# An FFN up projection by seven half products instead of eight, with the norm ahead of the products

## The chip, the cores and the metric

The kernel runs on one core of a Trainium2 chip. The metric is the device time of one execution in microseconds (us). The engines are TensorE (PE, with its weight loads PEld), VectorE (DVE), ScalarE (ACT), GpSimd (POOL) and SyncE (SP), whose queue issues nearly all DMAs.

## What is computed

Two layers of an encoder over 768 tokens, 512 of one sequence and 256 of another. A layer adds a merge of four gated branches to x, and then a feed-forward network (FFN) with a depthwise convolution of width 3 along the tokens:

```python
def rms_norm(x, g):
    xf = x.astype(jnp.float32)
    y = xf * lax.rsqrt(jnp.mean(xf * xf, axis=-1, keepdims=True) + EPS)
    return (y * g.astype(jnp.float32)).astype(x.dtype)

def conv_ffn(h, w_up, w_dw, b_dw, w_down):
    u = depthwise_conv(h @ w_up, w_dw, b_dw)
    a, b = jnp.split(u, 2, axis=-1)
    return (jax.nn.silu(a) * b) @ w_down
...
        x = x + merged @ w_out[l]
        x = x + conv_ffn(rms_norm(x, ffn_norm[l]), ffn_w_up[l], ffn_conv_w[l], ffn_conv_b[l], ffn_w_down[l])
```

The model has 1024 features, and the FFN 2816 for each of a and b. All is float32.

## The kernel before

**Layout.** Features lie on the 128 partitions and tokens along the free dimension; x, h and the products are 8 blocks of 128 features by 768 tokens. Sequence one has columns 0 to 511, sequence two 512 to 767. A float32 product is three products of parts: an operand is split into `hi` and `lo`, and `fm` issues for each block k of 128 features `wh` x `xh`, `wh` x `xl` and `wl` x `xh` (L377), each on 512 columns and then on 256 (`full`). So one output block of 128 features takes 8 x 3 x 2 = 48 matmuls, into a PSUM tile `mm` of two banks.

**Weights** are streamed in units of 512 columns (four blocks): SP loads `raw`, ScalarE casts it to `whi` (`put_hi`, L332), VectorE makes `wlo` (`put_lo`, L338). `pump` emits these when the main stream, whose advance in microseconds is estimated as products are emitted, says that they are due. Ten pairs and five raw tiles are held. Small work (side streams) is written as generators, whose steps are emitted in between products in the same way; an engine's queue then runs in the order of emission.

**Norm.** h is x times the gains, not normalised; `x_in` makes its parts and the sums of squares as x becomes final. The factor 1/rms of each token (`rbc`, in the rows as `ssq`) multiplies what the products give.

**FFN.** There are 22 pairs j: column block j gives a, column block 22 + j gives b. `ffn_half` makes one block: 48 matmuls, VectorE multiplies PSUM by `rbc` (L1208), ScalarE writes the middle tap and bias (L1201) into `u`, and VectorE adds the side taps (L1195, L1197) from PSUM, for each sequence in its turn. `ffn_glu` then makes silu(a) b: tanh on ScalarE, a VectorE step (L1235), GpSimd's product (L1236), and a split (L1238, L1240). The order of up groups and down products is `FF_ORDER`; a down product is done two up groups later than its up group where there are such (d0 after u1). `FF_GROUPS` are (0, 2), (2, 4), (6, 4), (10, 4), (14, 4), (18, 4). A down adds into x, which stays in SBUF (L1267); the last of a layer gives the next layer's h, or the output. `lagged` makes the last blocks of a product sequence one first, so that the next stage can start on it, and `ffn_first` starts on sequence one in the same way.

**Around it.** `proj_out` is the output projection ahead of the FFN. Its last five blocks go through `lagged`, each product in a small PSUM tile of its own.

Of the kernel before, what the change touches and what calls it, by code (L numbers as in the profile page):

```python
# [23 lines left out]
NFF = 22  # L24
FF_GROUPS = ((0, 2), (2, 4), (6, 4), (10, 4), (14, 4), (18, 4))
FF_ORDER = ("u0", "u1", "d0", "u2", "d1", "u3", "d2", "u4", "d3", "u5", "d4", "d5")
# [27 lines left out]
def layer_units(i, l):  # L54
# [34 lines left out]
    for step in FF_ORDER:  # L89
        j0, n = FF_GROUPS[int(step[1])]  # L90
        if step[0] == "u":
            for j in range(j0, j0 + n):
                out.extend(fu[j])
                out.extend(fu[NFF + j])
        else:
            w = wd[128 * j0:128 * (j0 + n)]
# [79 lines left out]

class Units:
    """The operands in the next n units of the weights, each w columns wide, taken from the stream when first asked
    for."""
# [16 lines left out]
class Net:  # L196
    """One pass through the layers. The large products (the main stream) are emitted in order; the rest of a
    branch (side streams) is written as generators whose steps are emitted between them, and a step's yield says
    how much of the main stream (in microseconds of the tensor engine) comes before its next one."""

    WB = 10
    RB = 5
    T_HI = 3.0
    T_LO = 0.7
    NB = 24

    def __init__(self, ctx, tc, depth, widths, xin, wu, mcd, fcd, mud, hcd, out):
# [15 lines left out]
        self.raws, self.his, self.ready = [], [], []  # L223
        self.nrm = {}

# [14 lines left out]
    def phase(self, name, ns, nmm):  # L240
        """The pools of a phase: ns small tiles, nmm of the wide PSUM tiles."""
# [56 lines left out]
    def drain(self, e=None):  # L298
        """Emit side steps until e is done (all of them without e)."""
# [6 lines left out]
    def pump(self):  # L306
        """Emit what is due: a unit's load, its hi part once the load should have come, then its lo part."""
        more = True
        while more:
            more = False  # L310
            if self.his and self.his[0][0] + self.T_LO <= self.now:
                self.put_lo()
                more = True
            if self.raws and self.live < self.WB and self.raws[0][0] + self.T_HI <= self.now:
                self.put_hi()
                more = True
            self.load_raw()

    def load_raw(self, most=RB):
        while self.di < self.depth * len(self.widths) and len(self.raws) + len(self.his) < most:  # L320
# [4 lines left out]
            self.raws.append((self.now, n, raw))  # L325
            self.di += 1

    def put_hi(self):
        _, n, raw = self.raws.pop(0)
        self.live += 1  # L330
        hi = self.pw.tile([128, n], F32R, tag="whi", name=self.nm("whi"), bufs=self.WB)
        self.nc.scalar.copy(hi, raw)  # L332
        self.his.append((self.now, n, raw, hi))

    def put_lo(self):
        _, n, raw, hi = self.his.pop(0)
        lo = self.pw.tile([128, n], F32R, tag="wlo", name=self.nm("wlo"), bufs=self.WB)
        self.nc.vector.tensor_sub(lo, raw, hi.bitcast(F32))  # L338
        self.ready.append((hi, lo))

    def unit(self):
        while not self.ready:
            if self.his:
                self.put_lo()
            else:
                self.load_raw()
                self.put_hi()
# [1067 lines left out]
```

## Time and profile before

| | |
|---|---|
| runs | 2823.68, 2825.2, 2837.93 us; median 2825.2 |
| span of the profiled execution, which is the time of that execution too | 2825.7 us |
| TensorE busy | 2788.8 us, 99% |
| VectorE busy | 1624.0 us, 57% |
| ScalarE busy | 949.5 us, 34% |
| GpSimd busy | 482.8 us, 17% |
| DMA, share of 16 engines | 20% |
| matmuls | 15676 with the transposes |

The page cuts the span in 40 slices and prints for each engine the busy share in tenths. The chain that ended last is followed back from the last instruction, at each step to what released it. Windows give busy times in stretches of the span with the granted clock of TensorE; the groups by form give count, busy time and mean duration of one kind of instruction; the timeline gives instructions in order of time.

### The profile page before, as it was taken

What the parts mean: (1) busy time and instruction counts of PE and PEld (TensorE: products, weight loads), DVE (VectorE), ACT (ScalarE), POOL (GpSimd) and SP (SyncE); (2) the same over time, 40 slices, a digit from 0 to 9 for tenths busy, and PEclk for the clock granted to TensorE, in tenths of its full rate; (3) what the DMA queues carried; (4) which work ended last, traced back from release to release, by engine and by line L of the source; (5) the groups of instructions that cost most, each with busy time, mean ns of one, the idle gap of its engine ahead of it and who ended that gap; (6) DMA issues with size and microseconds to landing.
All of it is one profiled execution on the core that took longest, in us unless ns stands there. A gap on an engine that the chain in (4) does not pass through costs nothing.

```text
span 2825.7 us, 39870 instructions
## 1 busy us (share of the span) xinstructions
PE 2788.8 (99%) x15676; PEld 2428.6 (86%) x15676; DVE 1624.0 (57%) x2804; ACT 949.5 (34%) x1929; POOL 482.8 (17%) x408
## 2 busy tenths in 40 slices
PE   9999999999999999999999999999999999999999
PEld 8778988888888888888787789888888888888888
DVE  6644438886445665555446443387874466655653
ACT  6443333223233332223344433342232333322330
POOL 3402113121121010000114021231121210100000
PEclk9999999999999999999999999999999999999999
DMA  5101113221132211221221011132212221212211
GB/s 166 42 27 38 41 47 114 61 67 60 60 105 62 67 64 60 64 64 56 81 91 42 27 38 31 57 110 64 62 62 64 90 75 61 68 60 68 64 59 58
DMA packets 110204, 183.35 MB, mean 65 GB/s; under 512 B 16321, under 2 KB 32065, under 8 KB 110017
## 3 DMA queue, kind: packets, MB, share of 16 engines
q1 hardware_dynamic: 110016, 180.81, 20.2%
q8 instruction: 123, 2.02, 0.3%
q14 instruction: 65, 0.52, 0.1%
HBM read 168.03 MB, written 11.16 MB: 63 GB/s over the span
## 4 chain that ended last, share of the span: by engine, by line
PE 94%; DVE 3%; POOL 1%; ACT 1%; issue 1%; DMA 0%; SPq 0%; ACTq 0%; DVEq 0%; POOLq 0%
PE mm L377 61%; PE mm L397 16%; PE ps L377 8%; PE ps L386 3%; PE ps L856 2%; PE ps L673 1%; PE ps L904 1%; PE ps L706 1%; PE ps L907 1%; POOL st L404 0%; DVE wlo L338 0%; PE ps L620 0%; PE ps L463 0%; PE ps L397 0%; PE ps L622 0%
## 5 line engine op out<-in xcount | busy, mean ns | idle before, releaser
L377 PE MATMUL mm<-hh,whi 128*128 128x256 f32 (+1 forms) x2560 | 668.0, 340 | 1.2 <-ACT whi L332 1.2
L332 ACT CAST whi<-raw 128x512 fp32r<-128x512 f32 (+1 forms) x576 | 354.3, 616 | 924.7 <-PE mm L377 779.2
L377 PE MATMUL mm<-hh,wlo 128*128 128x256 f32 (+1 forms) x2560 | 664.0, 338 | 0.0
L377 PE MATMUL mm<-hl,whi 128*128 128x256 f32 (+1 forms) x2560 | 661.7, 337 | 0.0
L338 DVE TENSOR_TENSOR wlo<-raw,whi 128x512 fp32r<-128x512 f32 (+1 forms) x576 | 419.7, 737 | 97.4 <-ACT whi L332 95.6
L377 PEld LDWEIGHTS mm<-hh,whi 128*128 128x128 f32 x2560 | 394.5, 188 | 60.8 <-issue 3.5
L377 PEld LDWEIGHTS mm<-hh,wlo 128*128 128x128 f32 x2560 | 393.8, 188 | 55.9
L377 PEld LDWEIGHTS mm<-hl,whi 128*128 128x128 f32 x2560 | 392.1, 188 | 55.9
L377 PE MATMUL mm<-b,whi 128*128 128x512 f32 (+1 forms) x1600 | 351.4, 339 | 7.0 <-DVE b L1151 6.2
L397 PE MATMUL mm<-whi,hh 128*128 128x512 f32 (+2 forms) x752 | 311.6, 414 | 7.3 <-ACT hh L422 6.1
L377 PEld LDWEIGHTS mm<-b,whi 128*128 128x128 f32 x1600 | 248.0, 190 | 46.4 <-DVE b L1151 4.9
L397 PE MATMUL mm<-whi,hl 128*128 128x512 f32 (+2 forms) x752 | 278.2, 370 | 0.0
L397 PE MATMUL mm<-wlo,hh 128*128 128x512 f32 (+2 forms) x752 | 277.7, 369 | 0.0
L1236 POOL TENSOR_TENSOR s<-s,s 128x768 f32<-128x768 f32 x44 | 91.3, 2076 | 890.6 <-DVE s L1235 890.6
L377 PE MATMUL mm<-b,wlo 128*128 128x512 f32 (+1 forms) x800 | 212.6, 340 | 0.0
L397 PEld LDWEIGHTS mm<-whi,hh 128*128 128x128 f32 x752 | 177.1, 235 | 29.2 <-issue 11.2
L404 POOL TENSOR_TENSOR st<-st,mhalf 128x16 f32<-128x16 f32 (+4 forms) x46 | 90.7, 1971 | 590.9 <-DVE st L781 372.3
L377 PE MATMUL ps<-b,whi 128*128 128x512 f32 (+1 forms) x832 | 189.7, 338 | 0.0
L397 PEld LDWEIGHTS mm<-wlo,hh 128*128 128x128 f32 x752 | 179.1, 238 | 11.8 <-issue 4.6
L397 PEld LDWEIGHTS mm<-whi,hl 128*128 128x128 f32 x752 | 177.4, 236 | 11.5 <-DVE hl L429 0.5
L1135 POOL TENSOR_TENSOR b<-b,b 128x768 f32<-128x768 f32 x48 | 99.8, 2078 | 462.3 <-DVE b L1130 437.4
L1008 DVE SCALAR_TENSOR_TENSOR b<-b,mc,b 128x497 f32<-128x497 f32 (+14 forms) x240 | 170.7, 760 | 0.1
(183 smaller groups left out, 3129.6 us busy)
## 6 DMA issues: line engine op xcount, KB each, us to landing
raw<-wu SPq DMA_DIRECT2D x560, 256.0 KB, 2.6
do<-ot SPq DMA_DIRECT2D x36, 132.0 KB, 2.4
b<-do SPq DMA_DIRECT2D x12, 384.0 KB, 3.5
raw<-wu SPq DMA_DIRECT2D x16, 208.0 KB, 2.8
b<-xin SPq DMA_DIRECT2D x8, 384.0 KB, 6.5
b<-xsp SPq DMA_DIRECT2D x8, 384.0 KB, 6.3
out<-b SPq DMA_DIRECT2D x8, 384.0 KB, 2.3
b<-xin SPq DMA_DIRECT2D x8, 256.0 KB, 5.0
```

Source lines behind the costliest of these rows:

```text
L332: self.nc.scalar.copy(hi, raw)
L338: self.nc.vector.tensor_sub(lo, raw, hi.bitcast(F32))
L377: nc.tensor.matmul(ap, w, x[:, c0:c1], start=(k == 0 and i == 0), stop=(k == K - 1 and i == 2))
L386: self.nc.tensor.transpose(out, x, self.ident)
L397: nc.tensor.matmul(ap, x[:, cols], w, start=(k == 0 and i == 0), stop=(k == 7 and i == 2))
L404: self.nc.gpsimd.tensor_tensor(r, ms, self.mhalf[:, 0:n], op=ALU.pow)
L673: nc.tensor.matmul(sc[:, 0:S], qkT[hh][:, 128 * t:128 * t + 128], qkT[4 + hh][:, 128 * t0:128 * t0 + S], start=True, stop=True)
L706: nc.tensor.matmul(sh["po"][:, hh, :], PT[:, 128 * kb:128 * kb + 128], v[(t0 + kb) // 3][:, (t0 + kb) % 3, 64 * hh:64 * hh + 64], start=(k ...
L856: nc.tensor.matmul(sc[:, x, y, 0:W], qT[y][rr, 128 * t:128 * t + 128], kT[y][rr, k0:k0 + W], start=True, stop=True)
L1008: nc.vector.scalar_tensor_tensor(acc[f][:, o0:o1], hc[f][:, o0 + d:o1 + d], w[:, 31 * f + k:31 * f + k + 1], acc[f][:, o0:o1], op0=ALU.mul ...
L1135: nc.gpsimd.tensor_add(a, a, t)
L1236: nc.gpsimd.tensor_mul(t, t, b)
```

## The change

**Seven products for eight.** Write the weights of a pair as blocks a11, a12 (column block j, features 0 to 511 and 512 to 1023) and a21, a22 (column block 22 + j), and h as b11, b21 (its two feature halves for columns 0 to 383) and b12, b22 (columns 384 to 767). A half product takes 4 blocks k of features on 384 columns: 12 matmuls. A pair takes eight of them in the usual way. `ffn_seven` takes seven, by Strassen's scheme in Winograd's form, on sums of weight blocks (s1 = a21 + a22, s2 = s1 + a11, s4 = s2 + a12, a21 + a11; the signs lie in the operands and in the last additions) and on operands T1 to T4 that are made once per layer from h:

```diff
+    def ffn_seven(self, j):
...
+        p = self.mm_ps()
...
+        X, Y = p[:, 0:HALF], p[:, 512:512 + HALF]
+        z1, z2 = self.s(NT), self.s(NT)
...
+        prod(X, b11)
+        nc.scalar.copy(z1[:, a], X)
+        prod(Y, b21)
+        nc.vector.tensor_add(z1[:, a], z1[:, a], Y)
+        self.ffn_rest()
+        Z = self.mm_ps()[:, 0:HALF]
+        prod(Z, self.tx["T1"])
+        nc.scalar.activation(z2[:, b], Z, AF.Identity, scale=-1.0)
+        prod(X, self.tx["T2"], True)
+        nc.scalar.copy(z1[:, b], X)
+        prod(Z, b22, True)
+        nc.vector.tensor_add(z1[:, b], z1[:, b], Z)
+        del Z
+        u1 = self.ffn_u(z1, j)
+        del z1
+        prod(X, self.tx["T3"], True)
+        nc.vector.tensor_sub(z2[:, b], z2[:, b], X)
+        self.rest = (j, X, z2, u1)
+
+    def ffn_rest(self):
...
+        self.fm(((X, 0, HALF),), self.units(1, 128), self.tx["T4"], 4, more=True)
+        self.nc.scalar.activation(z2[:, 0:HALF], X, AF.Identity, scale=-1.0)
+        del X
+        u2 = self.ffn_u(z2, NFF + j)
+        del z2
+        self.ffn_gate(j, u1, u2)
```

`more=True` goes on adding to what the PSUM tile holds. The last product of a pair, T4, is `ffn_rest`: it is issued in the next pair behind Y, or directly where a down product comes next. The results are put together in SBUF (`z1`, `z2`), and `ffn_u` makes the taps from there: `ffn_mid` (L1419 now) and `ffn_conv` (L1413, L1415 now) read SBUF. The lines of the PSUM steps are L1485 to L1509; the gate's VectorE steps are L1520 and L1525, GpSimd's product L1521.

**The order** is now a list; pairs 0 and 1 (`FF_PLAIN`) keep eight half products, 20 pairs per layer take seven:

```diff
-FF_ORDER = ("u0", "u1", "d0", "u2", "d1", "u3", "d2", "u4", "d3", "u5", "d4", "d5")
+FF_PLAIN = 2
+HALF = NT // 2
+
+FF_SEQ = (("u", 0), ("u", 1), ("u", 2), ("u", 3), ("d", 0, 2), ("u", 4), ("u", 5), ("u", 6), ("d", 2, 4), ("u", 7),
+          ("u", 8), ("u", 9), ("u", 10), ("d", 6, 4), ("u", 11), ("u", 12), ("u", 13), ("u", 14), ("d", 10, 4),
+          ("u", 15), ("u", 16), ("u", 17), ("u", 18), ("u", 19), ("d", 14, 4), ("u", 20), ("u", 21), ("d", 18, 4))
```

**Weights.** The stream gets a step between load and cast, a list of feeds; `L409` is the line of the sums, of which s1 and s4 are GpSimd's and the other two VectorE's. A pair that had four units of `hi` and `lo` has seven. The line of `put_hi` is L418 and that of `put_lo` L427. Eight pairs and six raw tiles are held, and three sums.

```diff
+        out += [
+            Feed("sum", a21, a22, s1, pool, last=a22),
+            Feed("sum", s1, a11, s2, dve, done=(s1,), last=a22),
+            Feed("sum", s2, a12, s4, pool, done=(s2, s4, a12), last=a22),
+            Feed("in", a21, a11, None, dve, done=(a21, a11), last=a22),
+        ]
```

**Norm ahead.** `hnorm_gen` waits for the sums of squares of 384 columns, makes `rbc`, and then for each k one VectorE product (L585), ScalarE's cast (L455) and VectorE's `lo` (L456). `t_gen` makes T1 to T4 in the same way, 16 operands, all emitted before pair 2; T2's difference is in part GpSimd's. `proj_out` works on halves of 384 columns, its last four blocks two to a PSUM tile, and calls `hnorm` after each half.

```diff
+        for k in range(8):
+            h = self.xs[k][:, cols]
+            nc.vector.scalar_tensor_tensor(h, h, g[:, k:k + 1], self.rbc[:, cols], op0=ALU.mult, op1=ALU.mult)
+            self.split(self.hs[k][0][:, cols], self.hs[k][1][:, cols], h)
+            yield 1.1
...
+        for k in range(4):
+            nc.vector.tensor_sub(x1[k][:, a], x1[k][:, a], x1[k][:, b])
+            t12[k] = self.b(dt=F32R), self.b(dt=F32R)
+            self.split(t12[k][0][:, a], t12[k][1][:, a], x1[k][:, a])
+            self.tx["T1"].append(tuple(t[:, a] for t in t12[k]))
+            yield 1.0
```

`ffn_plain` makes the first three column blocks half by half, with the results copied to SBUF (`flat`, L1433), and ends with `run_out`, which emits what is left of `t_gen`.

**x in DRAM.** The tiles of x hold h and its combinations during the FFN, so x goes to DRAM (`save_x`) after the projection and after each down, and a down loads it block by block into three buffers:

```diff
+                for m in range(8):
+                    if m < 7:
+                        load(m + 1)
...
+                    x = xr.pop(m)
+                    nc.vector.tensor_add(x, x, p[:, 0:NT])
+                    if last:
+                        nc.sync.dma_start(out=self.out[m], in_=x)
+                    else:
+                        self.go_fast(self.save_x(m, x, 0, NT), 1.5)
```

The last down of a layer issues the products of all but its last operand for some blocks first (`early`), and then waits for the side streams.

**Where instructions stand now.** VectorE in the middle of the first FFN, one column block of before: `mm` is the product in PSUM, `s` the small tiles with u, `b` x.

```order
L1208 TENSOR_TENSOR mm_8705<-mm_8705,ssq_7259 128x768
L1195 SCALAR_TENSOR_TENSOR s_8704<-mm_8705,fc_80,s_8704 128x511
L1197 SCALAR_TENSOR_TENSOR s_8704<-mm_8705,fc_80,s_8704 128x511
L1195 SCALAR_TENSOR_TENSOR s_8704<-mm_8705,fc_80,s_8704 128x255
L1197 SCALAR_TENSOR_TENSOR s_8704<-mm_8705,fc_80,s_8704 128x255
L338 TENSOR_TENSOR wlo_8781<-raw_8600,whi_8764 128x512
L1235 SCALAR_TENSOR_TENSOR s_8785<-s_8785,s_8630 128x768
L1267 TENSOR_TENSOR b_7278<-b_7278,mm_8774 128x768
```

No product of TensorE waits for one of these but through a free PSUM tile. VectorE after the change, at the end of a group, ahead of a down: s_9039 is `z1`, s_9040 `z2`, mm_9038 the tile of X, mm_9106 that of Z.

```order
L1495 TENSOR_TENSOR s_9039<-s_9039,mm_9106 128x384
L1413 SCALAR_TENSOR_TENSOR s_9169<-s_9039,fc_80,s_9169 128x511
L1415 SCALAR_TENSOR_TENSOR s_9169<-s_9039,fc_80,s_9169 128x511
L1413 SCALAR_TENSOR_TENSOR s_9169<-s_9039,fc_80,s_9169 128x255
L1415 SCALAR_TENSOR_TENSOR s_9169<-s_9039,fc_80,s_9169 128x255
L1525 SCALAR_TENSOR_TENSOR b_9105<-s_9117,b_9104 128x768
L427 TENSOR_TENSOR wlo_9182<-raw_9049,whi_9166 128x512
L1500 TENSOR_TENSOR s_9040<-s_9040,mm_9038 128x384
```

L1500, which reads T3's result out of X's tile, stands behind the taps of z1 and the gate's `lo` of the pair before. TensorE of before, where the up columns end and a down begins:

```order
L377 MATMUL mm_8705<-hl_7277,whi_8408 128x512
L377 MATMUL mm_8705<-hl_7277,whi_8408 128x256
L377 MATMUL mm_8705<-hh_7276,wlo_8424 128x512
L377 MATMUL mm_8705<-hh_7276,wlo_8424 128x256
L377 MATMUL mm_8774<-b_8052,whi_8446 128x512
L377 MATMUL mm_8774<-b_8052,whi_8446 128x256
```

The down goes into another PSUM tile. The same place after the change: `hh`, `hl` are T3's operands (they have taken the place of h's), `b_8263`, `b_8264` T4's.

```order
L472 MATMUL mm_9038<-hh_7258,whi_9007 128x384
L472 MATMUL mm_9038<-hl_7259,whi_9007 128x384
L472 MATMUL mm_9038<-hh_7258,wlo_9023 128x384
L472 MATMUL mm_9038<-b_8263,whi_9035 128x384
L472 MATMUL mm_9038<-b_8264,whi_9035 128x384
L472 MATMUL mm_9038<-b_8263,wlo_9047 128x384
```

T4's matmuls follow T3's, in the same PSUM tile, which L1500 reads in between. VectorE of before at the FFN's start, between the first two column blocks' second sequences and the next block (ssq is `rbc`):

```order
L1225 TENSOR_TENSOR mm_7901<-mm_7901,ssq_7259 128x256
L1195 SCALAR_TENSOR_TENSOR s_7899<-mm_7901,fc_80,s_7899 128x255
L1197 SCALAR_TENSOR_TENSOR s_7899<-mm_7901,fc_80,s_7899 128x255
L338 TENSOR_TENSOR wlo_8062<-raw_7879,whi_8046 128x512
L1235 SCALAR_TENSOR_TENSOR s_8066<-s_8066,s_7898 128x768
```

Only taps, gates and weights stand there. After the change, at the first pair with seven products, s_8279 is its `z1`, and L619 and L456 make T4's operands, the last of sixteen:

```order
L619 SCALAR_TENSOR_TENSOR b_7282<-b_7282 128x384
L456 TENSOR_TENSOR b_8272<-b_7282,b_8271 128x384
L427 TENSOR_TENSOR wlo_8287<-raw_7903,whi_8234 128x512
L1520 SCALAR_TENSOR_TENSOR s_8289<-s_8289,s_8128 128x768
L427 TENSOR_TENSOR wlo_8308<-raw_7832,whi_8297 128x512
L1487 TENSOR_TENSOR s_8279<-s_8279,mm_8278 128x384
```

L1487, the add of Y, stands behind all operands.

## Rows read from the trace of the kernel before

**Rows 1.** The page: span, shares and 40 slices of TensorE and its clock.

```profile
span 2825.7 us, 39870 instructions
PE 2788.8 (99%) x15676; PEld 2428.6 (86%) x15676; DVE 1624.0 (57%) x2804; ACT 949.5 (34%) x1929; POOL 482.8 (17%) x408
...
PE   9999999999999999999999999999999999999999
...
PEclk9999999999999999999999999999999999999999
```

**Rows 2.** The page: the chain that ended last, by engine and line.

```profile
PE 94%; DVE 3%; POOL 1%; ACT 1%; issue 1%; DMA 0%; SPq 0%; ACTq 0%; DVEq 0%; POOLq 0%
PE mm L377 61%; PE mm L397 16%; PE ps L377 8%; PE ps L386 3%; PE ps L856 2%; PE ps L673 1%; PE ps L904 1%; PE ps L706 1%; PE ps L907 1%; POOL st L404 0%; DVE wlo L338 0%; PE ps L620 0%; PE ps L463 0%; PE ps L397 0%; PE ps L622 0%
```

**Rows 3.** Windows in layer 1's FFN: length, busy (instructions) per engine, clock, DMA.

```profile
2280.00:2820.00 540.00, 539.58 (x3115) 471.37 (x3115) 306.82 (x432) 152.13 (x212) 45.64 (x22) 1.00 0.19 63
2640.00:2700.00 60.00, 60.00 (x348) 52.46 (x347) 32.06 (x44) 14.85 (x22) 4.00 (x2) 1.00 0.20 62
```

**Rows 4.** Timeline, `lagged` of layer 0's end: start, duration, engine, line, tiles.

```profile
1379.85 0.39 PE L377 MATMUL mm<-b,wlo 128*128 128x512 f32 x1
1380.27 0.69 DVE L1151 TENSOR_TENSOR b<-b,mm 128x512 f32<-128x512 f32 x1 [1.27 <-PE mm L377]
...
1381.02 0.50 PE L377 MATMUL mm<-b,whi 128*128 128x512 f32 x1 [0.78 <-DVE b L1151]
```

**Rows 5.** Groups by form, ScalarE: count, busy us, mean ns, idle before.

```profile
L332 ACT CAST whi<-raw 128x512 fp32r<-128x512 f32 x560 | 345.7, 618 | 905.8 <-PE mm L377 764.6 <-issue 63.3 <-PE mm L397 62.2
L1238 ACT ACTIVATE b<-s 128x768 fp32r<-128x768 f32 x44 | 37.2, 846 | 159.4 <-POOL s L1236 159.4
L629 ACT COPY b<-ps 128x384 f32<-128x384 f32 x12 | 5.7, 478 | 30.4 <-PE ps L620 30.4
```

**Rows 6.** Timeline of VectorE in layer 1's FFN, from a block's first side tap.

```profile
2598.68 0.75 DVE L1195 SCALAR_TENSOR_TENSOR s<-mm,fc,s 128x511 f32<-128x511 f32 x1 [1.06 <-ACT s L1201]
...
2601.04 1.28 DVE L338 TENSOR_TENSOR wlo<-raw,whi 128x512 fp32r<-128x512 f32 x2
```

**Rows 7.** Groups by form, VectorE.

```profile
L1235 DVE SCALAR_TENSOR_TENSOR s<-s,s 128x768 f32<-128x768 f32 x44 | 41.8, 951 | 0.0
L612 DVE TENSOR_TENSOR b<-b,st 128x384 f32<-128x384 f32 x24 | 16.2, 714 | 0.4 <-POOL st L404 0.4
L861 DVE TENSOR_TENSOR s<-ps,hc 128x384 f32<-128x384 f32 x16 | 8.9, 555 | 44.9 <-PE ps L856 44.9
```

**Rows 8.** Groups by form, GpSimd: the gate product, and a sum of 512 columns.

```profile
L1236 POOL TENSOR_TENSOR s<-s,s 128x768 f32<-128x768 f32 x44 | 91.3, 2076 | 890.6 <-DVE s L1235 890.6
L432 POOL TENSOR_TENSOR ssq<-ssq,s 128x512 f32<-128x512 f32 x28 | 37.5, 1339 | 141.0 <-ACT s L427 140.8
```

**Rows 9.** GpSimd beside L1008: timeline, the line's minimum/median/maximum there, and undisturbed form.

```profile
549.72 2.17 POOL L1135 TENSOR_TENSOR b<-b,b 128x768 f32<-128x768 f32 x1 [8.10 <-DVE b L1130]
...
L1008 DVE SCALAR_TENSOR_TENSOR b<-b,mc,b x3: 469/733/2331, 550.1 to 553.3; 128x508 f32<-128x508 f32 x1, 128x252 f32<-128x252 f32 x1, 128x507 f32<-128x507 f32 x1
...
L1008 DVE SCALAR_TENSOR_TENSOR b<-b,mc,b 128x505 f32<-128x505 f32 x8 | 5.9, 737 | 0.0
```

**Rows 10.** The page: DMA issues, KB each, median us to landing.

```profile
b<-do SPq DMA_DIRECT2D x12, 384.0 KB, 3.5
...
out<-b SPq DMA_DIRECT2D x8, 384.0 KB, 2.3
```

**Rows 11.** Window behind 1414 us, after gaps in `lagged`; the clock is third from the end.

```profile
1416.00:1421.00 5.00, 4.49 (x21) 4.19 (x21) 2.04 (x6) 1.93 (x5) 2.33 (x4) 0.50 0.51 150
```

More of the change, by code (lines that the diff above doesn't have):

```diff
@@ L174, in layer_consts, with __init__, layer_feeds, plain @@
     return c, f, np.concatenate([uq, ukv, sln, ws], axis=1)
+class Feed:
+    def __init__(self, out, a, b=None, name=None, eng=None, done=(), last=0):
+        self.out, self.a, self.b, self.name, self.eng = out, a, b, name, eng
+        self.done, self.last = done, last
+def layer_feeds(l, widths):
+    n = len(widths)
+    n_ff = sum(4 if x[0] == "u" else 2 * x[2] for x in FF_SEQ)
+    out, late = [], []
+    pool, dve = (lambda nc: nc.gpsimd), (lambda nc: nc.vector)
+    def plain(u):
+        return Feed("raw", u, done=(u,), last=u)
+    u = l * n
+    out += [plain(u + i) for i in range(n - n_ff)]
+    u += n - n_ff
+    for step in FF_SEQ:
+        if step[0] == "d" or step[1] < FF_PLAIN:
+            c = 2 * step[2] if step[0] == "d" else 4
+            out += late
+            late = []
+            out += [plain(u + i) for i in range(c)]
+            u += c
+            continue
+        a11, a12, a21, a22 = range(u, u + 4)
+        s1, s2, s4 = (f"s{x}_{u}" for x in (1, 2, 4))
+        out += [Feed("raw", a11, last=a11), Feed("raw", a12, last=a12)] + late
+        out += [
[4 more added lines that the diff above has]
+        ]
+        late = [plain(a22)]
+        u += 4
+    assert u == l * n + n and not late
+    return out
 class Units:
@@ L324, in load_raw, with can_sum, t_due @@
             self.nc.sync.dma_start(out=raw, in_=self.wu[l, i, :, 0:n])
-            self.raws.append((self.now, n, raw))
+            self.raws[self.di] = raw
+            self.t_raw[self.di] = self.now
             self.di += 1
+    def can_sum(self):
+        if self.fs >= len(self.feeds):
+            return False
+        f = self.feeds[self.fs]
+        return f.last < self.di and not (f.out == "sum" and len(self.sums) >= self.SB)
+    def t_due(self):
+        return self.t_raw[self.feeds[self.fs].last] + self.T_HI
@@ new lines, in put_src @@
+    def put_src(self):
+        f = self.feeds[self.fs]
+        if f.out == "raw":
+            self.src[self.fs] = self.raws[f.a]
+            self.t_src[self.fs] = self.now
+        else:
+            a = self.sums[f.a] if isinstance(f.a, str) else self.raws[f.a]
+            b = self.raws[f.b]
+            if f.out == "sum":
+                o = self.pw.tile([128, 512], F32, tag="sum", name=self.nm("sum"), bufs=self.SB)
+                self.sums[f.name] = o
+            else:
+                o = a
+            f.eng(self.nc).tensor_add(o, a, b)
+            self.src[self.fs] = o
+            self.t_src[self.fs] = self.now + self.T_SUM
+        self.fs += 1
@@ L376, in fm @@
                 for ap, c0, c1 in segs:
[L377 removed]
+                    nc.tensor.matmul(ap, w, x[:, c0:c1], start=(k == 0 and i == 0 and not more),
+                                     stop=(k == K - 1 and i == 2), skip_group_check=more)
             if rel and k % rel == rel - 1:
```

328 lines of the change are left out of this document (240 added, 88 removed).

## The prediction

> **What bounds the kernel now.** I read the page's shares and slices first: TensorE is busy 99% of the span, in every slice, at the full granted clock (2.4 GHz) [rows 1]. The chain that ended last says the same: 94% of it is matmuls, and the product helper's line L377 leads [rows 2]. Then the windows of the FFN: in 540 us TensorE idles 0.42 us, and Vector works 307 of them [rows 3]. So the FFN is bound by TensorE, and each matmul that is taken out is worth its time so long as TensorE stays fed. 60.00 us hold 348 matmuls, half of 512 columns and half of 256, so 172.4 ns for a mean of 384 columns [rows 3].
>
> Span and page are 2825.7, 0.5 above the median of 2825.2; the sum is made against 2825.7 and 0.5 comes off.
>
> **The saving.** A pair of up columns takes 4 x 4 x 3 x 2 = 96 matmuls of mean 384 columns, 16.55 us. Seven half products take 7 x 12 = 84 of 384 columns, 14.48 us (2.07 each). 40 pairs change, so TensorE's own work falls by 40 x 2.07 = **82.8 us**. What follows is what it waits for instead.
>
> **Y waits for the copy of X.** X and Y lie in one PSUM tile, and Y's first matmul waits for ScalarE's copy out of X's half. The nearest row is a product that waited for Vector to read its tile's other half: the matmul after it started 1.17 us later instead of 0.23, 0.94 lost [rows 4]. Scalar's copy of 384 columns is 478 ns against that add's 687 [rows 4, 5], so I take 0.72; between 0 (not waited for) and 0.94. Seven plus this wait: 15.20 us.
>
> **Vector's queue in one pair.** Per seven it runs 7 weight `lo` parts (two in 1.28 us [rows 6], so 4.48), two weight sums (1.28), three adds out of PSUM (0.555 each [rows 7], 1.67), eight side taps (four in 2.36, from 2598.68 to 2601.04 [rows 6]; 4.72) and two gate operations (0.951 [rows 7]; 1.90): **14.05 us**. So far it fits under 15.20. Two things come on top. The side taps now read both inputs from SBUF while GpSimd runs: s1 and s4 (about 1.34 each) and the gate product of 2.08 [rows 8]. The trace has that meeting: a 508-wide operation of two SBUF inputs, started at 550.10 while a GpSimd product of 2.17 ran from 549.72, took 2331 ns where 505 columns take 737 undisturbed [rows 9], so 1.59 is lost. I charge one such loss for the gate product and 0.9 for s4. And the taps of z1 wait until Scalar has made the middle tap, which stands behind a `hi` cast of 0.85 and a weight cast of 0.62 [rows 5]: 1.2. The period is then 14.05 + 1.59 + 0.9 + 1.2 = **17.75 us**; it replaces 15.20, since T2 waits for Vector's add of Y and T4 for its subtraction L1500 (the order of Vector's queue above). From below 15.6 (14.05 with one loss), from above 19.3 (both sums lose 1.59 and the middle tap 0.4 more).
>
> By the Trainium skill ("SBUF — State Buffer", Who interferes with whom), a Vector instruction with two SBUF inputs contends with a GpSimd instruction that reads SBUF and the later comer waits for all of it; one with at most one SBUF input does not. It speaks against this change, which moves the taps' input from PSUM to SBUF; by it all 4.76 us of GpSimd could stand in Vector's way instead of my 2.49, which is the third rival below. The 1.59 lost of 2.17 [rows 9] agrees with it.
>
> **The end of a group.** Before each down product T4 follows T3 directly. T4 needs L1500, and in Vector's queue that stands behind the add of Z, four taps, the gate's `lo` and a weight's `lo`. From the end of b22: add 0.555, middle tap 0.85, taps 2.36, 0.95, 0.64, L1500 0.555, with hand-overs of 0.2 at four places 6.7; T3 covers 2.07 of it. So TensorE stands still **at least 4.6 us**, 12 times (55 us), and longer when Vector comes late: with a last period of 17.2 it is 6.9.
>
> **The groups.** After a down the first seven takes 13.2; X, the wait and Y of the next, 4.86; T4 2.07: T4 of the first ends at 20.1. A group of n ends at 20.1 + 17.75 (n - 2) + 17.2, against 16.55 n before: +4.2 for n = 2, +5.4 for 3, +6.6 for 4, +7.8 for 5. A layer has 2, 3, 4, 4 and 5 behind its first down: **+30.6**. These numbers hold the saving already.
>
> **From the output projection to the first down.** Here h is normalised before any product can start. One k is a Vector product (0.714, the row of two SBUF inputs), Scalar's cast (0.478) and Vector's `lo` (0.555) in a row: 1.75 [rows 5, 7]. Count from the end of the projection's first half. The first half's chain (add, square, GpSimd's sum, small matmuls, power, broadcast, copy) takes about 6.2, an estimate from rows of 0.5 to 1.7 each; eight k's with four `lo` parts and two adds between them end at 24.0, and the last add of the second half stands in Vector's queue behind seven of them, at 22.2. The second chain then ends at 22.2 + 6.2 + 14.0 = 42.4, and the third plain column at 42.4 + 0.5 + 8.3 = 51.2; TensorE's work till there is 41.3. Next come the operands T1 to T4, all emitted ahead of j = 2, and T2 of j = 2 waits for the add of Y behind all of them: copies and taps 5.0, T1 7.0, T2 7.0, T3 2.2, T4 7.0, with taps, gate, sums and `lo` parts between 8.5, so **36.7 us**, of which 14.4 lie beside TensorE's fourth column, X and Y. Then 28.1 remain to the down. 51.2 + 36.7 + 28.1 = 116.0 against 16.55 x 5 = 82.8: **+33.2 per layer**. Between +20 (k's at 0.555 for the product, and operands that overlap) and +42 (GpSimd's losses in each k).
>
> **x in DRAM.** Per down eight loads and eight saves of 384 KB join SP's queue, with 3.5 and 2.3 us [rows 10] against 4.1 us of TensorE per block where n = 4: nothing, hidden by the block before. In d(0,2) a block has 2.07 and three buffers turn in about 6.8: I charge 1.5 per layer (0 to 5). Layer 0's and 1's ends, with operands needed at once: 1.5 each.
>
> **The clock.** After TensorE idled and waited around 1414 us, the granted clock was 0.50 (1.2 GHz) there, and 21 matmuls of 256 columns took 4.49 us where they take 2.5 [rows 11]. The stalls of 5 to 22 us above are longer than the gaps there. 12 times 1.7, so **20 us**; 0 to 40.
>
> **Sum.** 2 x (30.6 + 33.2) + 2 x 3 + 20 = 154 on 2825.7: 2979, less 0.5. **2979 us.**
>
> **The rivals.**
> (a) TensorE stays the bound: **faster**. Place: the add of Y, the copy of X and L1500 come through Vector's queue without a wait. For it: Vector's 14.05 lies under 15.20 and it has 43% of the span free today. Against it: the chain of 6.7 at a group's end. The price: 40 x 0.2 for Y, 12 x 2 for T4, 10 per layer for the start: 8 + 24 + 20 - 82.8 = -31, so 2794. It decides from the point where all added waits lie under 2.07 per pair.
> (b) Vector's queue holds only its own sum: the period is 15.6 and the last one 14.95 (stall 4.6), the start +20, no clock loss. Groups come to +2.4 per layer: 2 x (2.4 + 20 + 1.5) + 2825 = 2873; with half of the clock loss and +28 at the start, 2900.
> (c) GpSimd's ports and the long start weigh more: period 19.3, last 18.7, start +42, clock 40: 2 x (50.7 + 42 + 1.5) + 40 + 2825 = 3053.
> (d) It does not do what it says: products are fewer but as slow as before, with the waits hidden: near 2825.
>
> **How the numbers follow.** My forecast (2930 to 3015) 0.53; (b), 2860 to 2930, 0.21; (c), 3015 to 3090, 0.15; (a) 0.07; (d) 0.04. The range takes in the bounds 2873 and 3053: 2872 to 3055. Faster by over 0.5% (14 us, about what a measurement of this kernel can tell from none) 0.07, within it 0.04, slower 0.89.
>
> **What would show it.** In the changed profile TensorE's share falls to about 90% and its idle time names Vector: L1487, L1500, L585/L456 and the copy L1485. The matmul of Y after X starts 0.5 to 0.9 late, 40 times; before each down there is a gap of 5 to 7 us; T2 of j = 2 has a gap of some 22 us; T4 to T4 within a group takes 17 to 18 us. If Vector idles between its rows while TensorE works, (a) or (b) is right; if the taps of 511 take 2 us where GpSimd runs, (c). Wrong would be the forecast if the chain at a group's end is under 4 us, or if the operands T1 to T4 are made at under 1.2 us per k.

## The result

The changed kernel takes **3071.7 us** (3068.4 to 3073.4) against 2824.4: 1.086 of the time before (95% interval 1.083 to 1.089). The forecast was 2979, with a range of 2872 to 3055. The sign was right, and the time lies 17 us above the range.

The page of the changed kernel, in the form of [rows 1]: span, shares, and the slices of TensorE and of its clock.

```profile
span 3068.7 us, 40394 instructions
PE 2775.4 (90%) x15196; PEld 2487.2 (81%) x15196; DVE 1837.2 (60%) x3118; ACT 1097.9 (36%) x2245; POOL 622.3 (20%) x496
...
PE   9999999999974798898899999999999757988988
...
PEclk9999999999997999999999999999999979999999
```

TensorE's share has fallen from 99 to 90%, as forecast. The hole does not lie evenly in the FFN: in each layer there is one slice with 7, one with 4 or 5 and another with 7, at the FFN's start, and from there on 8 and 9.

TensorE's waits by releaser (us in total, times, longest us):

```profile
PE mm L472 <- ACT s L1485: 113.1, 40, 33.5
PE mm L472 <- DVE s L1500: 98.0, 28, 10.4
PE mm L472 <- DVE b L1379: 20.5, 10, 5.8
PE mm L472 <- DVE xr L1571: 9.4, 6, 3.5
```

L1485 is the copy of X, for which Y waits (40 times, as forecast), L1500 the subtraction for which T4 waits, L1379 the adds in the output projection's halves, L1571 the add of a down. Windows in both FFNs, in the form of [rows 3] (540 us, busy us per engine, clock, DMA):

```profile
900.00:1440.00 540.00, 433.58 (x2355) 404.36 (x2354) 365.14 (x516) 204.24 (x334) 103.93 (x60) 0.93 0.32 104
2430.00:2970.00 540.00, 434.17 (x2351) 404.73 (x2350) 363.67 (x516) 204.67 (x335) 104.52 (x60) 0.93 0.31 103
```

TensorE idles 106 us of 540, where it idled 0.4 before [rows 3].

**Where the 243 us are** that lie between the two profiled executions (3068.7 and 2825.7). The stretch ahead of the first FFN runs the same work in all kernels, but its end (the last cast ahead of the projection) lies between 784.0 and 790.6 us in 13 profiles. To be free of that, I count from there: before 2041.6 us to the end, the changed kernel 2278.9, so **+237**. Within that, by the starts of a down's last add in layer 1 (2557.74, 2865.09 and others in the timeline) against before's pace of 99.8 us for four pairs and a down:

| layer 1 | before, same work | after | difference | forecast |
|---|---|---|---|---|
| projection to the first down's end (4 pairs) | 153.5 | 235.4 | **+81.9** | +36.4 |
| 3 pairs and down | 83.2 | 89.9 | +6.7 | +7.1 |
| 4 pairs and down | 99.8 | 109.2 | +9.4 | +8.3 |
| 4 pairs and down | 99.8 | 108.3 | +8.5 | +8.3 |
| 5 pairs and down | 116.4 | 127.7 | +11.3 | +9.5 |
| 2 pairs and the layer's end | 66.5 | 71.2 | +4.7 | +7.4 |

(The forecast's column takes its clock term, 1.7 per stall, and its 1.5 for the ends into the rows.) The five groups come to +40.6 where +40.6 was forecast; to the tenth that is luck, since the rows miss by up to 2.7 either way. In layer 0 the start costs +83 and the groups about +31: before takes 101.8 us there for four pairs and a down (why is open), the changed kernel 107.6 and 108.2, no more than in layer 1. So it is the FFN's start that was missed, by 45 us or a little more in each layer.

**A pair inside a group.** Each takes 17.4 us:

```profile
1382.60:1400.00 17.40, 15.12 (x84) 14.48 (x84) 15.60 (x23) 8.96 (x16) 4.45 (x2) 1.00 0.19 62
```

VectorE is busy 15.6 of the 17.4. From the timeline of the second half of this pair, by engine:

```profile
1391.45 2.94 DVE L427 TENSOR_TENSOR wlo<-sum,whi 128x512 fp32r<-128x512 f32 x2
1394.31 0.54 DVE L1495 TENSOR_TENSOR s<-s,mm 128x384 f32<-128x384 f32 x1
1396.19 0.75 DVE L1413 SCALAR_TENSOR_TENSOR s<-s,fc,s 128x511 f32<-128x511 f32 x1 [1.34 <-ACT s L1419]
...
1393.87 0.85 ACT L1523 ACTIVATE b<-s 128x768 fp32r<-128x768 f32 x1 [3.22 <-POOL s L1521]
...
1391.61 2.23 POOL L1521 TENSOR_TENSOR s<-s,s 128x768 f32<-128x768 f32 x1 [4.88 <-DVE s L1520]
```

GpSimd's gate product starts at 1391.61. The two weight parts on VectorE beside it take 2.94 where two take 1.28 undisturbed [rows 6]: 1.66 lost, where I had charged 1.59 (on the taps, which come later). The Trainium skill ("SBUF — State Buffer", Who interferes with whom) names VectorE's second SBUF input as what meets GpSimd's reads; the 1.66 agree.

VectorE then waits 1.34 for the middle tap of z1 (L1419). Scalar's cast L1523, which waits for GpSimd, stands ahead of that tap, but it is not what makes the wait: the tap needs the add of Z, and with the cast behind the tap (x8) VectorE still waits 1.10, as it does without GpSimd's product (x7, x11). The cast has 0.24 of it.

**Ahead of a down**, T3's last matmul and T4's first:

```profile
1410.99 0.34 PE L472 MATMUL mm<-hh,wlo 128*128 128x384 f32 x1
1418.00 1.01 PE L472 MATMUL mm<-b,whi 128*128 128x384 f32 x2 [6.67 <-DVE s L1500]
```

7.01 us from start to start, so 6.8 lost; 6.9 were forecast.

**The FFN's start** in layer 0. First the chain from the last add of the projection's first half (838.80) to the first normalised block:

```profile
838.80 0.55 DVE L1379 TENSOR_TENSOR b<-b,mm 128x384 f32<-128x384 f32 x1 [4.61 <-PE mm L472]
...
840.10 1.03 POOL L550 TENSOR_TENSOR ssq<-ssq,s 128x384 f32<-128x384 f32 x1 [4.16 <-ACT s L548]
842.24 0.72 PE L564 MATMUL ps<-ones,ssq 128*128 128x1 f32 x6
843.00 0.16 DVE L567 TENSOR_SCALAR st<-ps 128x3 f32<-128x3 f32 x1 [0.95 <-PE ps L564]
843.24 0.87 POOL L503 TENSOR_TENSOR st<-st,mhalf 128x3 f32<-128x3 f32 x1 [2.11 <-DVE st L567]
844.72 1.46 DVE L573 TENSOR_SCALAR s<-hc,st 128x128 f32<-128x128 f32 x3
848.01 0.81 PE L576 MATMUL ps<-s,ones 128*128 128x384 f32 x2
850.45 0.46 ACT L580 COPY ssq<-ps 128x384 f32<-128x384 f32 x1
850.95 1.17 DVE L585 SCALAR_TENSOR_TENSOR b<-b,fc,ssq 128x384 f32<-128x384 f32 x1 [0.40 <-ACT ssq L580]
```

12.1 us, and the second half's chain (866.97 to 879.34) 12.4, where 6.2 were forecast. The steps take 6.6 us; between them stand gaps of up to 1.8 us, above all around the small matmuls, which take their turn among TensorE's products: GpSimd's sum ends at 841.1 and L564 starts at 842.24, the diagonal is done at 846.2 and L576 starts at 848.01. The product of the projection's second half halts meanwhile, since the add for which it waits stands in VectorE's queue behind the blocks:

```profile
853.19 0.34 PE L472 MATMUL mm<-b,wlo 128*128 128x384 f32 x1
859.37 1.01 PE L472 MATMUL mm<-b,whi 128*128 128x384 f32 x2 [5.85 <-DVE b L1379]
```

Then the operands. Y of the first pair waits for the copy of X:

```profile
946.89 0.51 ACT L455 CAST b<-b 128x384 fp32r<-128x384 f32 x1 [1.09 <-DVE b L619]
...
948.57 0.47 ACT L1485 COPY s<-mm 128x384 f32<-128x384 f32 x1
...
949.09 0.69 PE L472 MATMUL mm<-hh,whi 128*128 128x384 f32 x1 [33.47 <-ACT s L1485]
```

X was done at 915. Its copy stands in Scalar's queue behind the sixteenth operand's cast (946.89), so TensorE stands still for 33.5 us.

### The profile page after: what moved, and what is told of

Its sections match the earlier page's. It is cut to its first block, busy times and chain, and to the rows that moved or that the text cites. A ratio compares the mean times of both kernels' runs of the same rounds, so it can differ in the third digit from the quotient of the medians.

```text
span 3068.7 us, 40394 instructions
## 1 busy us (share of the span) xinstructions
PE 2775.4 (90%) x15196; PEld 2487.2 (81%) x15196; DVE 1837.2 (60%) x3118; ACT 1097.9 (36%) x2245; POOL 622.3 (20%) x496
## 5 line engine op out<-in xcount | busy, mean ns | idle before, releaser
L472 PE MATMUL mm<-b,whi 128*128 128x512 f32 (+2 forms) x2880 | 702.6, 348 | 135.6 <-DVE s L1500 98.0
L472 PE MATMUL mm<-hh,whi 128*128 128x384 f32 (+2 forms) x1920 | 568.8, 346 | 125.7 <-ACT s L1485 113.1
L418 ACT CAST whi<-raw 128x512 fp32r<-128x512 f32 (+1 forms) x576 | 352.1, 614 | 839.2 <-PE mm L472 657.8
L472 PEld LDWEIGHTS mm<-b,whi 128*128 128x128 f32 x2880 | 501.0, 195 | 183.7 <-DVE s L1500 107.0
L472 PE MATMUL mm<-hl,whi 128*128 128x384 f32 (+2 forms) x1920 | 555.7, 339 | 0.9 <-DVE hl L456 0.8
L472 PE MATMUL mm<-hh,wlo 128*128 128x384 f32 (+2 forms) x1920 | 556.3, 340 | 0.0
L427 DVE TENSOR_TENSOR wlo<-raw,whi 128x512 fp32r<-128x512 f32 (+1 forms) x576 | 451.2, 790 | 89.8 <-ACT whi L418 89.0
L472 PEld LDWEIGHTS mm<-hh,whi 128*128 128x128 f32 x1920 | 324.7, 190 | 172.0 <-ACT s L1485 126.3
L472 PE MATMUL mm<-b,wlo 128*128 128x384 f32 (+2 forms) x1440 | 433.6, 344 | 0.0
L472 PEld LDWEIGHTS mm<-hh,wlo 128*128 128x128 f32 x1920 | 324.0, 190 | 24.5
L472 PEld LDWEIGHTS mm<-b,wlo 128*128 128x128 f32 x1440 | 256.4, 195 | 15.8
L503 POOL TENSOR_TENSOR st<-st,mhalf 128x16 f32<-128x16 f32 (+5 forms) x50 | 94.1, 1882 | 600.8 <-DVE st L968 376.7
L1413 DVE SCALAR_TENSOR_TENSOR s<-s,fc,s 128x511 f32<-128x511 f32 (+1 forms) x176 | 108.2, 615 | 170.2 <-ACT s L1419 170.2
L1521 POOL TENSOR_TENSOR s<-s,s 128x768 f32<-128x768 f32 x44 | 91.4, 2078 | 512.1 <-DVE s L1520 502.2
```

Source lines behind the costliest of these rows:

```text
L472: nc.tensor.matmul(ap, w, x[:, c0:c1], start=(k == 0 and i == 0 and not more), stop=(k == K - 1 and i == 2), skip_group_check=more)
L503: self.nc.gpsimd.tensor_tensor(r, ms, self.mhalf[:, 0:n], op=ALU.pow)
L1413: nc.vector.scalar_tensor_tensor(u[:, c0 + 1:c1], z[:, 0:n - 1], w[:, 3 * col:3 * col + 1], u[:, c0 + 1:c1], op0=ALU.mult, op1=ALU.add)
L1521: nc.gpsimd.tensor_mul(t, t, b)
```

## The experiments

All runs below are the changed kernel with one edit, unless said. Each was executed once, but x9 four times. The differences are taken from the start of the last cast ahead of the first projection to the end of the span, so that the stretch ahead of it drops out; the changed kernel's 2278.9 is what they stand against. The stage between the two FFNs, which no edit touches, still takes 773.9 to 778.6 us in these profiles (777.9 in the changed kernel; 3 to 4 us less in x1, x4 and x9), so a difference of under some 5 us says nothing.

| run | time, us | from the first FFN on | against the changed kernel |
|---|---|---|---|
| x1 operands not made | 3010.9 | 2222.8 | -56 |
| x2 no statistics | 3048.8 | 2256.0 | -23 |
| x3 eight products | 2877.1 | 2090.3 | -189 |
| x4 T4 within the down | 2990.6 | 2200.0 | -79 |
| x5 Y apart | 3041.3 | 2253.1 | -26 |
| x6 operands earlier | 3037.1 | 2247.1 | -32 |
| x7 no gate product | 3020.6 | 2230.0 | -49 |
| x8 gate's cast later | 3062.1 | 2276.0 | -3 |
| x9 x4, x5 and x6 together | 2946.6 (median) | 2155.2 | -124 |
| x10 no GpSimd sums | 3054.0 | 2266.9 | -12 |
| x11 GpSimd silent | 3006.3 | 2217.3 | -62 |

**x1: the operands T1 to T4 not made.**

```diff
-        e = [self.now + 0.5, self.t_gen()]
-        self.fast.append(e)
+        a, b = slice(0, HALF), slice(HALF, NT)
+        pick = lambda ks, c: [tuple(t[:, c] for t in self.hs[k]) for k in ks]
+        self.tx = {"T1": pick(range(0, 4), a), "T2": pick(range(0, 4), b),
+                   "T3": pick(range(0, 4), b), "T4": pick(range(4, 8), a)}
...
-        self.run_out(e)
```

> The operands T1 to T4 are not made: the four products take slices of the normalised h in their place (this leaves out that part of the computation), with all else as in the changed kernel. Theory: what the forecast missed lies at the FFN's start, where Y of the first pair waits 33.8 us for a copy that stands on ScalarE behind all operands' casts. Then that gap falls to 1 to 2 us, the 10.6 us stall ahead of the first down to about 7, and the low clock behind them goes: about 40 us per layer, 2990 us. Rival (the operands cost the 22 us per layer that were forecast, and the rest of the miss is spread over the groups): about 3027 us.

28 us per layer, between the two. The gap of 33.5 fell to 6.1, not to 1 or 2: what is left is the copies and taps of three plain columns, which also stand ahead. And the stall of 10.4 ahead of the first down did not move, so it has another cause than the operands (x10 tests it):

```profile
PE mm L472 <- DVE s L1502: 98.1, 28, 10.4
PE mm L472 <- ACT s L1487: 58.4, 40, 6.1
```

**x2: the norm without statistics.**

```diff
-            nc.vector.scalar_tensor_tensor(h, h, g[:, k:k + 1], self.rbc[:, cols], op0=ALU.mult, op1=ALU.mult)
+            nc.vector.scalar_tensor_tensor(h, h, g[:, k:k + 1], h, op0=ALU.mult, op1=ALU.mult)
```

with the small matmuls, the power, the diagonal and the copy L580 left out ahead of it.

> The norm multiplies by the gains and by x itself, and does not wait for the sums of squares, the small products and the power (this leaves out the norm's factor; the sums of squares are still made). Theory: each of the two chains from the last add to the first normalised block takes 12 us, twice what was forecast, and nearly all of it goes: TensorE's stalls of 6.0 and 2.4 us in the projection's second half shrink and the plain columns' second half starts some 12 us earlier; 13 us per layer, about 3045 us. Rival (the pace of 1.67 us per block on VectorE and ScalarE sets the start, whenever it begins): under 6 us per layer, about 3060 us.

11 us per layer, near the 13 of the theory, though not by both chains. The edit takes them out whole, 24.5 us, and not only the two times 6 by which they were mis-sized. The blocks of the first half start 8 us earlier, but the last add of the projection comes no earlier (77 us behind the cast in both kernels), so the gain is the second chain's. The halt in the projection stays, as 7.0 us in one piece:

```profile
860.60 0.69 PE L472 MATMUL mm<-b,whi 128*128 128x384 f32 x1 [7.02 <-DVE b L1358]
```

There the theory was wrong: that halt comes from the adds' place behind the blocks in VectorE's queue, not from the statistics.

**x3: eight products, with all else.** `ffn_eight` is the plain column's code for both blocks of a pair:

```diff
+            self.fm(self.halves(p), self.units(2, 128), self.hs, 4)
+            us.append(self.ffn_u(self.flat(p), col))
```

> All 22 pairs take eight half products; the norm ahead of the products, the halves of 384 columns, taps from SBUF, and x in DRAM stay. Theory: only the norm's start is left, about 19.5 us of TensorE's idle time per layer and some clock, and x in DRAM costs nothing: about 2870 us. Rival (taps from SBUF and x in DRAM cost time in every group): over 2900 us.

48.6 us above before from the first FFN on, 24 per layer: the norm ahead of the products, with x in DRAM. Its waits name the start; the down's add of the loaded x has 11 us of them in the whole kernel:

```profile
PE mm L473 <- DVE b L1380: 20.5, 10, 5.9
PE mm L473 <- DVE xr L1578: 11.0, 8, 3.4
PE mm L473 <- DVE b L1339: 7.6, 8, 1.4
```

Four pairs and a down take 100.5 and 99.2 us in layer 1, where before takes 99.8, so taps from SBUF cost nothing where VectorE has room. From the projection to the first down's end each layer has +34, against the changed kernel's +82. Of the +237, 49 belong to the norm and x, and 189 to the seven products with their operands and sums, which take 83 us of matmuls away: 272 us of waits and low clock came with them.

**x4: T4 within the down.**

```diff
-            self.ffn_rest()
             n = step[2]
...
+                    if not last and m == 8 // n:
+                        self.ffn_rest()
```

and its weights' place in the list of feeds.

> T4 of a group's last pair is issued behind the down's first two weight units, in all downs but a layer's last. Theory: the stall ahead of a down (6.8 us, 10.6 ahead of the first, and about 1.2 us of low clock each) lies beside the down's products: about 10 x 8 = 80 us less, 2990 us. Rival (VectorE's queue is late in itself, and the down's first blocks wait for their PSUM tiles instead): 40 us less or under, about 3030 us.

79 us less, as the theory has it: ten stalls of 6.8 to 10.4 us and their clock. T4's waits for L1500 (named L1502 here) fall from 98.0 to 23.8:

```profile
PE mm L474 <- DVE s L1502: 23.8, 18, 6.7
...
PE mm L474 <- DVE b L1527: 12.9, 6, 2.1
```

The rival's wait is there, but small: 12.9 us in six downs for the gate's `lo` of the down's operand.

**x5: Y in a PSUM tile of its own.**

```diff
-        X, Y = p[:, 0:HALF], p[:, 512:512 + HALF]
+        X, Y = p[:, 0:HALF], self.ps()[:, 0:HALF]
```

> Y gets a PSUM tile of its own, so its first matmul does not wait for ScalarE's copy of X. Theory: VectorE's queue sets the period of 17.4 us inside a group, so the 1 to 1.8 us go to another wait of the same pair; only the first pair of a group and the FFN's start gain, together 15 to 25 us: about 3050 us. Rival (the hand-over of the PSUM tile is a cost by itself): all 40 waits go, 45 us without the FFN's starts: about 3020 us or less.

38 of the 40 waits for the copy are gone, and 26 us. Inside a group two pairs take 35.28 us, 17.6 each, where they took 17.4 (17.3 to 18.8 over all groups):

```profile
1346.84:1382.12 35.28, 31.30 (x170) 30.66 (x170) 31.18 (x44) 18.18 (x31) 10.60 (x5) 0.95 0.20 61
...
1386.93 0.68 PE L472 MATMUL mm<-b,whi 128*128 128x384 f32 x2 [2.57 <-DVE s L1500]
```

The wait has moved to T4, and nothing is gained there. The gain is in a group's first pairs, and at the FFN's start, where Y and T1 now lie within the long gap (25.3 us): the gap is 8 us shorter, and the first down ends 5 and 3 us earlier. In the steady pairs VectorE sets the period.

**x6: the operands earlier.**

```diff
             self.finish(c0)
+            if c0:
+                e = [self.now + 0.5, self.t_gen()]
+                self.fast.append(e)
...
+        if self.te:
+            self.run_out(self.te[0])
         self.ffn_rest()
```

with T3 and T4 in a second generator, run out ahead of the product with T3.

> The order of emission alone: T1 and T2 are made beside the plain columns' second halves, T3 and T4 behind X and Y of the first pair. Theory: what costs at the FFN's start is the place of the operands in the queues, ahead of the copy of X, more than their number; the gap of 33.8 us falls to 8 or less: 25 to 30 us per layer, about 3015 us. Rival (VectorE and ScalarE need these 40 us for 16 operands wherever they stand): about 10 us per layer, 3050 us.

16 us per layer, between the two again. The gap at Y is 6.0 (5.0 in layer 1):

```profile
927.60 0.69 PE L472 MATMUL mm<-hh,whi 128*128 128x384 f32 x1 [6.00 <-ACT s L1492]
```

but a plain column now waits 7.5 and 8.0 us for its tile's copy. So at least 16 of the operands' 28 us per layer (x1) come from their place; how much of the other 12 is the work itself is open, since the new wait is one of place again.

**x7: no gate product on GpSimd.**

```diff
-        nc.gpsimd.tensor_mul(t, t, b)
```

> GpSimd's product of the gate (2.2 us) is left out, so silu(a) goes on without its factor b (this leaves out that part of the computation). Theory: GpSimd's product makes the period longer twice, by VectorE's weight part beside it (2.3 us for 0.7) and by ScalarE's cast that waits for it ahead of the middle tap (3.2 us idle); the period falls from 17.4 to under 16 us and the stalls ahead of a down by about 1 us: 45 to 65 us, about 3015 us. Rival (the period is VectorE's own 14 us plus TensorE's hand-overs, whatever GpSimd does): within 15 us of 3071.

49 us, within the theory's sum, but not by its parts: two pairs take 33.22 us, 16.6 each, where it said under 16, and the stall ahead of a down falls by 1.9 (6.67 to 4.78):

```profile
1344.34:1377.56 33.22, 30.25 (x169) 28.97 (x169) 30.05 (x48) 18.34 (x30) 6.34 (x3) 1.00 0.21 65
```

**x8: the gate's cast later.**

```diff
         nc.gpsimd.tensor_mul(t, t, b)
-        yield 3.0
+        yield 6.0
```

> The gate's cast on ScalarE is emitted 3 us of the main stream later, so that it stands behind the middle tap of z1 instead of ahead of it, and the gate's last VectorE step behind L1500; all work and GpSimd's product stay. Theory: the wait of ScalarE for GpSimd leaves the path, VectorE's contention stays: the period falls from 17.4 to about 16.2 us, the chain ahead of a down gets 0.95 us shorter: 40 to 50 us, about 3025 us. Rival (contention on VectorE is all of it): within 15 us of 3071.

A miss: 3 us, which is no difference. The stall ahead of a down is 5.6 for 6.7, and some pairs take 17.0, but not 16.2, and as many take 18.5. Scalar's late cast now stands directly ahead of the copy of X, and Y waits 2.11 us in the steady pairs, where it waited 1.63. Of two pairs in a row the first has the low clock behind that wait, the second not:

```profile
1361.31:1379.86 18.55, 16.44 (x84) 16.12 (x84) 15.59 (x23) 9.08 (x15) 6.15 (x3) 0.91 0.19 58
1379.86:1396.85 16.99, 14.86 (x84) 14.54 (x84) 15.61 (x23) 9.08 (x15) 4.45 (x2) 1.00 0.21 63
```

The rival's number came out, and most of its reason: VectorE's wait for the middle tap only falls from 1.34 to 1.10, so Scalar's wait for GpSimd was never the 1.2 us that the theory took away:

```profile
1377.71 0.75 DVE L1413 SCALAR_TENSOR_TENSOR s<-s,fc,s 128x511 f32<-128x511 f32 x1 [1.10 <-ACT s L1419]
```

**x10 and x11: GpSimd's sums, and GpSimd altogether.**

```diff
...
-            f.eng(self.nc).tensor_add(o, a, b)
+            if not (f.out == "sum" and f.name[1] in "14"):
+                f.eng(self.nc).tensor_add(o, a, b)
```

> GpSimd's two weight sums of a pair are left out (the raw block goes on in their place, so this leaves out part of the weights' sums); VectorE's two sums and GpSimd's gate product stay. Theory: the stall of 10.6 us ahead of the first down is long since VectorE's sum s2 waits 3.25 us for GpSimd's s1, behind the gate product, and the add of Z stands behind it; it falls to about 7, and VectorE's weight part beside s4 loses its 0.6 us per pair: about 25 us, 3045 us. Rival (the first pair is late by its operands): the 10.6 stays, under 15 us in all.

> GpSimd's weight sums and its gate product are both left out (these parts are not computed). Theory: VectorE's own 14.05 us per pair then lie under TensorE's 15.2, so the period inside a group falls to 15.2 to 15.8 us and only the start, the hand-over to Y and the chain ahead of each down (about 5 us) stay: about 2990 us. Rival (VectorE's queue is behind by its own order): the period stays over 16.3 us, 3005 us or more.

x11 is this edit and x7's together. The stall ahead of the first down falls from 10.43 to 7.67, as x10's theory says:

```profile
975.35 1.01 PE L475 MATMUL mm<-b,whi 128*128 128x384 f32 x2 [7.67 <-DVE s L1503]
```

In the changed kernel VectorE's sum of a weight that is needed only after the down waits for GpSimd's, and the add of Z, which TensorE needs, stands behind it:

```profile
977.79 1.27 POOL L409 TENSOR_TENSOR sum<-raw,raw 128x512 f32<-128x512 f32 x1
...
979.10 0.69 DVE L409 TENSOR_TENSOR sum<-sum,raw 128x512 f32<-128x512 f32 x1 [3.25 <-POOL sum L409]
...
982.58 0.54 DVE L1495 TENSOR_TENSOR s<-s,mm 128x384 f32<-128x384 f32 x1
```

The whole gain, 12 us, is half of what was expected, and under the 15 that the rival gave: the pairs inside a group stay at 17.4, so the sums cost nothing there beside the gate product. Without the gate product they do, since 16.6 (x7) become 15.75 with GpSimd silent, within the theory's 15.2 to 15.8:

```profile
1340.63:1356.38 15.75, 14.84 (x86) 14.52 (x85) 13.44 (x23) 9.19 (x15) 0.00 (x0) 1.00 0.22 68
```

TensorE's 14.5 and the hand-over to Y are then nearly all of it. GpSimd costs 1.65 us per pair in all. The time, 3006, is above the 2990 that I gave and at the rival's 3005, though not by the rival's period: the first down ends only 10 us earlier per layer, and ahead of each down 5.1 us are left from start to start, where there were 7.0:

```profile
1387.65 0.69 PE L475 MATMUL mm<-b,whi 128*128 128x384 f32 x1 [4.78 <-DVE s L1503]
```

**x9: x4, x5 and x6 together.**

> The three edits of order and place together: T4 behind the first units of a down, Y in a PSUM tile of its own, T1 and T2 beside the plain columns and T3 and T4 behind X and Y. All is computed. Theory: they take away waits at different places, so their single gains of 81, 34 and 30 us add up but for the first pair's copy of X, which two of them share (some 15 us per kernel): about 2940 us, still above the kernel before, since VectorE's period of 17.4 us and the norm's chains stay. Rival (with one wait gone VectorE is late at the next): 2970 us or more.

2946.6 us, 1.043 of before (1.039 to 1.047). The three single gains, 79, 26 and 32, add up to 137, and 124 came; nothing new takes their place. What keeps it above before is the FFN's start: from the projection to the first down's end it still has +53 and +55. All that follows is level with before in layer 0 (-1 us) and 9 above it in layer 1. So with T4 and Y placed otherwise the groups about break even: what a pair saves and what it still waits for nearly cancel. The waits that are left:

```profile
PE mm L474 <- DVE s L1514: 51.6, 18, 6.7
PE mm L474 <- DVE b L1386: 21.2, 10, 5.9
PE mm L474 <- ACT s L1502: 16.0, 2, 8.0
PE mm L474 <- ACT s L1440: 15.4, 2, 7.8
```

No version here beats the kernel before.

## Why the prediction was wrong in size and right in sign

**Right: the bound before, the saving, and near enough the period and the stall.** The saving, 40 x 2.07, was read from a window at TensorE's full rate, and is there: 84 matmuls have 14.5 us. The period (17.75 forecast, 17.4 measured) and the stall ahead of a down (6.9 and 6.8) came near what was worked out from the order of VectorE's queue and the durations of before's rows; the groups' +40.6 is layer 1's alone. x5 shows that VectorE and not the tile's hand-over sets the period, x7 and x11 that GpSimd's part is 1.65 us, and x4 that the stalls are worth 79 us.

Within the period the shares were not all right, and their errors partly cancel, so the nearness of its size is in part luck. VectorE's own work is 13.4 us (x11) and not 14.05, what GpSimd adds to it 2.2 and not 2.49, VectorE's idle time 1.8 and not 1.2. The 1.59 for the gate product fell on a weight's part, not on the taps. The 0.9 for s4 is no term of its own: the period stays when the sums go (x10). The 1.2 for the middle tap was put down to two casts ahead of it, but it is the time from the add of Z over the tap itself (x8). And the upper bound of 19.3 does not follow from its words: with 1.59 for the gate product and for each sum they give 20.4.

**Wrong: "From the output projection to the first down".** It was +33.2 per layer with an upper bound of +42, and measured +82 with its clock. (The forecast's +36.4 in the table above has its clock and x in it.) By its own steps, in layer 0, counted like there from the end of the projection's first half (838.4):

| step | forecast | measured |
|---|---|---|
| third plain column done | 51.2 | 65.1 |
| from there to T2 of the first pair | 36.7 | 52 |
| from there to T4's end | 28.1 | 37 |
| the down | 18.0 | 22 |

- The chains ahead of the blocks, "about 6.2, an estimate from rows of 0.5 to 1.7 each", took 12.1 and 12.4. I added the steps and left out the turns: four engines hand over nine times in a row, and two of the steps are small matmuls that wait behind products in TensorE's queue. The last add of the second half comes at 28.6 instead of 22.2 and that half's blocks end at 54.4 instead of 42.4, 12 us late. A run shows the second chain's part alone: x2, without both chains, has the fourth column 10 us earlier, but the last add no earlier.
- The pace per block was right (1.75 forecast; 1.67 from 881.01 to 882.68).
- The operands: I let X, Y and the fourth column lie beside them ("14.4 lie beside"), since I named only VectorE's add of Y as what T2 waits for. But Y already waits for Scalar's copy of X, and that copy stands behind all operands' casts. So Y and T1 came after the 33.5 us, at the low clock, instead of within them. I had named that wait, Y for the copy, and priced it at 0.72 everywhere, without asking what stands ahead of the copy in Scalar's queue at the first pair. The copies and taps ahead of the operands took 10 us (903.6 to 913.7) and not 5.0, since there are three columns of them, and T1 and T2 themselves took longer than 7.0, with GpSimd's differences and gate product beside them.
- The stall ahead of the first down is 10.4 and not 4.6: the weight's sum that waits for GpSimd (x10).
- The upper bound took the same sum with longer operations. It did not ask what else could stand ahead of each step, and so it was no bound.

**The clock.** 20 us were forecast. Start-to-start times of the matmuls give about 40 us lost at 1.2 GHz in the two FFNs and their projections, against some 4 in the same stretches of before. The window from 940 to 960, behind the longest gap, has a granted clock of 0.63:

```profile
940.00:960.00 20.00, 10.91 (x47) 10.91 (x48) 11.17 (x20) 7.82 (x15) 2.21 (x1) 0.63 0.09 27
1060.00:1080.00 20.00, 13.33 (x69) 12.83 (x68) 12.10 (x17) 8.75 (x15) 3.51 (x2) 0.83 0.39 131
```

The stall ahead of a down (the second line) costs 1.0 to 1.6 us by it; 1.7 was taken.

**x in DRAM.** 1.5 per layer forecast; 9.4 us of waits in the whole kernel, 3.5 at the first down where a load comes late. Three times the forecast, and small still.

**The rivals.** (a), TensorE stays the bound, would need the period of 15.75 that only a silent GpSimd gives, and no chain ahead of a down. (b), at 2873, has the start at +20 and the period at 15.6, and neither is there. (c), at 3053, is nearest in number: its long start came, at twice its +42, and its 40 us of clock, but its period of 19.3 is not there. (d) falls with the 14.5 us for 84 matmuls.

**What stays open.** The steps above, read from the trace, place 42 of the some 45 us that were missed per layer. The runs do not divide them: x1 and x2 take 39 us per layer off the start and x10 some 3 off the stall, but of the whole +82, with what was forecast, and they were not taken away together. Why the first stretch's end varies by 6 us between executions is open, and so is why before is 2% slower in layer 0's FFN than in layer 1's.

## What to carry to other kernels

A product saved is worth its time only if the other engines can hand over its inputs and outputs without keeping TensorE waiting. Work that fits by its sum is not enough: here each pair gave VectorE about 14 us of work, GpSimd about 5 and TensorE 14.5, and 2.07 us saved per pair bought 6.8 of waits and low clock (272 us for 83 in all, the start with them). Where the products stand counts as much as how many there are: x9 makes the same products and takes 124 us less. When an order of emission changes, price each wait by what stands ahead of its releaser in the releaser's own queue, at each different place, and above all at the first use, where the one-time work is emitted; the price of the steady place says nothing of that. A chain over several engines costs its hand-overs and its turns in each queue, so take its length from a like chain of the trace, from first start to last, and not from the sum of its steps.

## What the runs showed that was not expected

VectorE's weight part (512 columns, two SBUF inputs) beside GpSimd's gate product lost as much as the taps were expected to lose: 2.94 us for two instead of 1.28. In x5 a stall of 2.57 us inside a group was followed by the low clock: the window of two pairs there has a granted clock of 0.95, while the changed kernel's pair with two waits of under 2 us keeps 1.00. In x8 a wait of 2.11 us was followed by it in one pair (0.91, 18.55 us) and not in the next (1.00, 16.99 us), so that a wait that is half a microsecond longer can cost a pair 1.5 us more.
